# Complex tables of an S5 branch as three wide real products, with roots spread tile by tile and small loads moved to the start

## The chip, the cores and the metric

The kernel runs on one core of one Trainium2 chip, in float32 throughout (matmul operands split into a high and a low part of type float32r, three matmuls for one product). The metric is the device time of one execution in microseconds, the median of several runs. The change is judged by the same time of the changed kernel.

## The reference

One bidirectional encoder layer over two sequences of 512 tokens (the kernel sees them as 1024 rows), D = 1024. The parts that the change touches are the first norm, the u projection and the tables of the state-space branch:

```
h = rms_norm(x, ln1);  q, k, v, u, g_att, g_ssm = split(h @ w_in)
# S5 branch: 2 directions, 64 groups, 64 states, 16 channels a group
dt = exp(log_dt);  A = exp((lam_re + i lam_im) * dt)          # complex, one per (direction, group, state)
B_bar = (A - 1) / lam * (b_re + i b_im)                        # complex, (direction, group, state, 16)
h_t = A * h_(t-1) + B_bar u_t      (forward and backward scan over 512 steps)
y = Re(C h) + d_skip * u
# attention: windowed, with a relative bias by bucket of (key - query): bias = rel_table[bucket]
```

After it come gelu and a gated product, the merge with the attention branch, an output product with residual, a second norm and a squared-ReLU MLP. The change alters none of the results, only how some are reached.

## The kernel before, in words

The scan over 512 steps is cut into 64 chunks of T = 8 steps (`NCHUNK`). For each group the kernel builds, from powers of the complex A, a table `bpre` (B_bar times A^0 to A^7: what a chunk's inputs add to the state) and a table `ctab` (C times A^0 to A^8: what a state adds to the outputs of a chunk, and the lag kernel of a chunk with itself). Real and imaginary part are two planes; the two directions lie in partitions 0 to 63 and 64 to 127.

The stages, in order:

- **Start.** SP loads four rows of x (`x_rows`), two weight columns (`uw_raw`), the transposed x (`x_columns`), then the second sequence. ACT squares each row (`row_root`, L278), POOL takes the power -1/2 of the mean (L280, L281). `spread(s)` (L283 to L289) turns four roots into a 128 x 512 tile of PSUM, where each row holds the root of each token: DVE makes a diagonal of each root, PE multiplies it with ones. `scaled` (L291) multiplies a column of xT by `ln1` and by that tile and splits it in two parts (ACT L296, DVE L297). PE then makes u columns 0 and 1 (L356), with the order of PE, ACT and DVE written by hand (`manual_schedule`). Before that loop DVE computes `dt`, the angle `ang` and its reduction, and the two low parts `uw_lo` of the first weight column, and only then `spread(0)`; `spread(1)` stands at the seam of the two sequences.
- **Powers.** After the loop: sine, exponential, the powers `pr`, `pi` of A by doubling (L379 to L388), the factors `fr`, `fi`, and ten copies on ACT (L402 to L406) into `er`, `ei`, `br_p`, `bi_p`, where each direction has its order of powers.
- **Tables** (`tables(c)`, c = 0 to 7, eight groups each, in two turns q of four groups), with `u_column(2)` and `(3)` ahead and four more u columns between. For each c: SP loads b and c; DVE makes `bb` with negated planes beside it, ACT writes `lbt`. For each turn, six DVE instructions (L474 to L476, twice) make `bpre` and six (L482 to L484, twice) make `ctab`, which goes to `ct_scr` in DRAM. PE multiplies `lbt` with `ctab` (L493, the lag kernel) into a bank of `sps`, ACT copies it to `ks` (L497). SP loads `u_sb`. For each pair of groups PE transposes `bpre` (L506), ACT copies it to `bm` (L508), PE multiplies it with `u_sb` (L513) into another bank of `sps` (two in all), and ACT copies that into the states `h` (L518, L519). At the end of a c DVE adds d_skip on the diagonal (`dg`, L521 to L523) and SP stores `ks` in three transfers to `lag_scr`.
- **Gates and scan.** PE multiplies 13 gate columns (`Gate.whole`, L166, 48 matmuls each); DVE runs the scan over the chunks (L643 to L649, 62 steps of four instructions). After the second gate the bias line is made (one matmul of `rel` with a one-hot, L547) and written to DRAM for all queries (`line_scr`). POOL builds `toep_scr` from `lag_scr` (L554).
- **Read-out** (L741 on): 32 turns, each with loads of `u_sb`, `toep` and `ctab_in` five turns ahead, six matmuls (L686, L688) and a share of three late gates and of the key projection, in an order written by hand.
- Attention, merge and MLP follow, untouched.

Where no order is written, the framework's scheduler orders each engine's queue ahead of the run from its own estimate; at run time each queue (PE, ACT, DVE, POOL, SP) runs in that order, and an instruction that waits holds all behind it. A tile's pool has a number of buffers; the next writer of a buffer waits for the last reader.

Of the kernel before, what the change touches and what calls it, by code (L numbers as in the profile page):

```python
# [63 lines left out]
def hybrid_layer(ctx, tc, x, xT, rel, onehot, ln1, w_qkv, w_ug, q_gain, k_gain, sink, lam_re, lam_im, log_dt,  # L64
# [27 lines left out]
    ct_scr = dram.tile([P, GROUPS, 2, 9 * CH], F32, name="ct_scr")  # L92
# [113 lines left out]
    er = cf.tile([P, 9, GROUPS], F32, name="er")  # L206
    ei = cf.tile([P, 9, GROUPS], F32, name="ei")
    br_p = cf.tile([P, T, GROUPS], F32, name="br_p")
    bi_p = cf.tile([P, T, GROUPS], F32, name="bi_p")
# [3 lines left out]
    lbt = cf.tile([P, 2, SB, 48], F32, name="lbt")  # L213
    with tc.tile_pool(name="xin", bufs=2, reuse_waits="tile") as xin, tc.tile_pool(name="ssmc", bufs=1) as sc:
# [25 lines left out]
        x_rows(0)  # L240
        for c in range(2):
# [6 lines left out]
        SP.dma_start(dd[32:48, :], d_skip)  # L248
        SP.dma_start(bglu_sb, b_glu)
# [33 lines left out]
        def spread(s):  # L283

            ps = spread_ps[s] = sps()
            for i in range(4):
                dg = xin.tile([P, P], F32, tag="rs_diag", name="rs_diag", bufs=4)
                V.tensor_scalar_mul(dg, ident, root[s * 4 + i])
                PE.matmul(ps[:, i * P:(i + 1) * P], ones, dg, start=True, stop=True)  # L289
# [25 lines left out]
        with tc.manual_schedule(engines={mybir.EngineType.PE, mybir.EngineType.Activation, mybir.EngineType.DVE}):  # L315
            exp_exact(dt, ldt)
            den, nr, tn = c64("den"), c64("nr"), c64("tn")
            V.tensor_mul(den, lr, lr)
            V.tensor_mul(tn, li, li)
            V.tensor_add(den, den, tn)  # L320
            V.reciprocal(den, den)
            V.tensor_mul(ang, li, dt)
            V.tensor_scalar(kk, ang, 1.0 / (2.0 * math.pi), ROUND_MAGIC, op0=ALU.mult, op1=ALU.add)
            V.tensor_scalar_add(kk, kk, -ROUND_MAGIC)
            for part in (TWO_PI_1, TWO_PI_2, TWO_PI_3):
                V.scalar_tensor_tensor(ang, kk, -part, ang, op0=ALU.mult, op1=ALU.add)
            V.tensor_scalar(ang, ang, -3.1415925, 3.1415925, op0=ALU.max, op1=ALU.min)
            for t in range(4):
                row_root(t)
            w_los = [weight_half(raw[:, i * KT // 2:(i + 1) * KT // 2, :], w, i) for raw, w in first_w for i in range(2)]  # L330
            w_los.pop(0)()
            w_los.pop(0)()
            spread(0)
            owed = [scaled(0, 0)]
            out_ps = {}
            for s in range(NSEQ):
                for c in range(2):
                    out_ps[c, s] = acc()
                for k in range(KT):
                    if k + 1 < KT:  # L340
                        owed.append(scaled(s, k + 1))
                    elif s == 0:
                        spread(1)
# [14 lines left out]
            for fn in w_los:  # L358
                fn()
            sn, sh = c64("sn"), c64("sh")  # L360
# [40 lines left out]
            for src, e_t, b_t in ((pr, er, br_p), (pi, ei, bi_p)):  # L401
                S.copy(e_t[0:64, 0:8, :], src[0:64, 1:9, :])  # L402
                S.copy(e_t[64:128, 0:8, :], src[64:128, 8:0:-1, :])
                S.copy(e_t[:, 8, :], src[:, 0, :])
                S.copy(b_t[0:64, :, :], src[0:64, 7::-1, :])
                S.copy(b_t[64:128, :, :], src[64:128, 0:8, :])  # L406
        for c in range(2):
            u_store(c, ups[c])
        V.tensor_scalar_mul(gain_q, gain_q, HD ** -0.5)
        V.tensor_scalar_mul(nsink, nsink, -1.0)  # L410
# [4 lines left out]
    if True:  # L415
# [4 lines left out]
        for ri in range(2):  # L420
            for s in range(NSEQ):
                for half, n in ((slice(0, 64), 7), (slice(64, 128), 0)):
                    S.copy(a8r[half, ri, :, s], er[half, n, :])
                    S.activation(a8i[half, ri, :, s], ei[half, n, :], AF.Copy, scale=-1.0 if ri == 0 else 1.0)
# [10 lines left out]
        with tc.tile_pool(name="ssmt", bufs=2) as sp:  # L435
            def tables(c):
# [3 lines left out]
                bx = sp.tile([P, 3, SB, CH], F32, tag="bx", name="bx")  # L440
                cx = sp.tile([P, 3, SB, CH], F32, tag="cx", name="cx")
                SP.dma_start(bx[:, 1], b_re[:, gs, :])
                SP.dma_start(bx[:, 2], b_im[:, gs, :])
                SP.dma_start(cx[:, 0], c_re[:, gs, :])
                SP.dma_start(cx[:, 1], c_im[:, gs, :])
                bb = sp.tile([P, 3, SB, CH], F32, tag="bb", name="bb", bufs=1)
                tw = sp.tile([P, 2, SB, CH], F32, tag="tb", name="tw", bufs=1)
                V.tensor_scalar_mul(bx[:, 0], bx[:, 2], -1.0)
                V.tensor_mul(tw, bx[:, 0:2], fi[:, None, gs, None].to_broadcast([P, 2, SB, CH]))
                V.tensor_mul(bb[:, 1:3], bx[:, 1:3], fr[:, None, gs, None].to_broadcast([P, 2, SB, CH]))  # L450
                V.tensor_add(bb[:, 1:3], bb[:, 1:3], tw)
                V.tensor_scalar_mul(bb[:, 0], bb[:, 2], -1.0)
                V.tensor_scalar_mul(cx[:, 1], cx[:, 1], -1.0)
# [1253 lines left out]
```

## Time and profile before

| | |
|---|---|
| median of 3 runs | 1565.12 us (1564.83 to 1565.55) |
| profiled execution, device time | 1567.3 us |
| its span, first to last instruction | 1565.5 us |
| mean granted TensorE clock | 0.988 |
| busy PE / PEld / DVE / ACT / POOL | 1489.8 / 1270.1 / 1125.5 / 769.1 / 125.4 us |

PE is TensorE's matmuls, PEld its weight loads, DVE VectorE, ACT ScalarE, POOL GpSimd, SP the queue that issues most transfers. A row of the groups reads: line, engine, operation, output and inputs, shapes, number of instructions, busy us, mean ns of one, then the engine's idle time just before them and what ended it. A float32 matmul appears as two passes.

### The profile page before, as it was taken

The numbers are of one execution on the slowest core, as the hardware profiler recorded it, in microseconds if no ns is written. First come the engines' busy times: TensorE is split into PE (matmuls) and PEld (weight loads), VectorE is DVE, ScalarE is ACT, GpSimd is POOL, SyncE is SP. The second block draws the span as 40 slices with busy tenths as digits, with TensorE's granted clock in tenths as the row PEclk, the third lists the DMA queues.
The fourth block names the chain that finished last, engine by engine and source line by source line (L and its number), as shares of the span: only waits on it lengthen the run. The fifth ranks groups of instructions, "written<-read, shape, count | busy, mean of one in ns | idle before, by whom it ended". The sixth has DMA issues, their size and how long they took to land.

```text
span 1565.5 us, 22224 instructions
## 1 busy us (share of the span) xinstructions
PE 1489.8 (95%) x8058; PEld 1270.1 (81%) x8058; DVE 1125.5 (72%) x2015; ACT 769.1 (49%) x1379; POOL 125.4 (8%) x222
## 2 busy tenths in 40 slices
PE   5999999999999999999899998999999999999998
PEld 3777778888999888897689986888888788888787
DVE  6898987995454888888784577777777578566553
ACT  5577763214334877777443344555455434433332
POOL 1000002000022233331100100000000000000000
PEclk9999999999999999999899998999999999999999
DMA  7443549427852332224954232444444694455332
GB/s 258 127 146 124 156 138 298 145 94 254 259 191 60 89 95 62 83 84 151 304 203 176 81 115 101 155 149 148 151 158 155 233 346 143 152 159 163 121 121 67
DMA packets 122713, 243.38 MB, mean 155 GB/s; under 512 B 16315, under 2 KB 47163, under 8 KB 122604
## 3 DMA queue, kind: packets, MB, share of 16 engines
q1 hardware_dynamic: 97564, 186.24, 37.5%
q10 hardware_dynamic: 22480, 46.25, 7.9%
q0 software_dynamic: 2560, 9.48, 1.9%
q8 instruction: 63, 1.03, 0.3%
q14 instruction: 46, 0.38, 0.1%
HBM read 172.68 MB, written 81.82 MB: 163 GB/s over the span
## 4 chain that ended last, share of the span: by engine, by line
PE 71%; DVE 15%; ACT 5%; DMA 4%; issue 3%; SPq 0%; POOL 0%; ACTq 0%; DVEq 0%
PE bank L128 13%; PE bank L129 13%; PE bank L127 13%; PE acc L593 5%; PE acc L622 5%; PE acc L166 4%; PE acc L128 2%; PE acc L127 2%; PE acc L129 2%; PE sps L688 2%; DMA c_raw<-in_w_ug_dram 2%; PE sps L493 2%; PE acc L356 2%; PE sps L513 1%; DVE h L649 1%
## 5 line engine op out<-in xcount | busy, mean ns | idle before, releaser
L127 PE MATMUL bank<-b_hi,a_hi 128*128 128x512 f32 x448 | 174.4, 392 | 3.9 <-ACT b_hi L1581 3.9
L128 PE MATMUL bank<-b_lo,a_hi 128*128 128x512 f32 x448 | 175.7, 392 | 2.1 <-DVE b_lo L1582 2.0
L129 PE MATMUL bank<-b_hi,a_lo 128*128 128x512 f32 x448 | 175.3, 391 | 0.0
L593 PE MATMUL acc<-w_hi,hT 128*128 128x256 f32 x768 | 165.0, 292 | 0.0
L166 PE MATMUL acc<-hT,c_hi 128*128 128x512 f32 x512 | 164.0, 397 | 0.0
L1581 ACT CAST a_hi<-d_a 128x1024 fp32r<-128x1024 f32 x56 | 58.9, 1052 | 182.0 <-PE bank L128 178.0
L1582 DVE TENSOR_TENSOR a_lo<-d_a,a_hi 128x1024 fp32r<-128x1024 f32 x56 | 68.5, 1224 | 107.3 <-ACT a_hi L1581 107.3
L593 PEld LDWEIGHTS acc<-w_hi,hT 128*128 128x128 f32 x768 | 128.0, 190 | 3.5
L166 PEld LDWEIGHTS acc<-hT,c_hi 128*128 128x128 f32 x512 | 96.2, 189 | 20.4 <-issue 1.5
L593 PE MATMUL acc<-w_lo,hT 128*128 128x256 f32 x384 | 108.6, 283 | 0.2 <-DVE w_lo L588 0.2
L127 PE MATMUL bank<-act,u_hi 128*128 128x512 f32 x256 | 101.1, 395 | 7.1 <-DVE a L1422 7.1
L127 PEld LDWEIGHTS bank<-b_hi,a_hi 128*128 128x128 f32 x448 | 84.5, 189 | 21.8 <-ACT b_hi L1581 4.3
L128 PEld LDWEIGHTS bank<-b_lo,a_hi 128*128 128x128 f32 x448 | 84.6, 189 | 21.1 <-DVE b_lo L1582 3.6
L166 PE MATMUL acc<-hT,c_lo 128*128 128x512 f32 x256 | 101.2, 395 | 0.0
L128 PE MATMUL bank<-act,u_hi 128*128 128x512 f32 x256 | 100.8, 394 | 0.0
L129 PE MATMUL bank<-act,u_lo 128*128 128x512 f32 x256 | 100.7, 393 | 0.0
L129 PEld LDWEIGHTS bank<-b_hi,a_lo 128*128 128x128 f32 x448 | 84.6, 189 | 17.5
L882 ACT ACTIVATE p<-p,nmx 128x257 f32<-128x257 f32 (+1 forms) x128 | 72.2, 564 | 35.8 <-DVE nmx L876 35.7
L1434 ACT CAST u_hi<-s 128x512 fp32r<-128x512 f32 x64 | 39.8, 623 | 74.4 <-PE bank L128 53.3
L593 PEld LDWEIGHTS acc<-w_lo,hT 128*128 128x128 f32 x384 | 73.4, 191 | 1.0 <-DVE w_lo L588 0.4
L876 DVE CUSTOM_DVE_ANT_0 p<-sps,bias,nsink 128x256 f32<-128x256 f32 (+1 forms) x128 | 69.1, 541 | 2.1 <-PE sps L872 0.3
L1582 DVE TENSOR_TENSOR b_lo<-k,b_hi 128x1024 fp32r<-128x1024 f32 x56 | 68.2, 1218 | 1.1 <-ACT b_hi L1581 1.1
(333 smaller groups left out, 3763.4 us busy)
## 6 DMA issues: line engine op xcount, KB each, us to landing
d_a<-a_scr SPq DMA_DIRECT2D x56, 512.0 KB
u_raw<-in_w_up_dram SPq DMA_DIRECT2D x32, 512.0 KB
a_scr<-t ACTq DMA_DIRECT2D x64, 256.0 KB
k<-in_w_down_dram SPq DMA_DIRECT2D x32, 512.0 KB
a_scr<-a ACTq DMA_DIRECT2D x48, 256.0 KB
c_raw<-in_w_ug_dram SPq DMA_DIRECT2D x44, 256.0 KB
ct_scr<-ctab SPq DMA_DIRECT2D x16, 576.0 KB
ctab_in<-ct_scr SPq DMA_DIRECT2D x32, 288.0 KB
```

The lines of the kernel that those rows point to most:

```text
L127: PE.matmul(ps, a[0], b[0], start=first, stop=False)
L128: PE.matmul(ps, a[0], b[1], start=False, stop=False)
L129: PE.matmul(ps, a[1], b[0], start=False, stop=last)
L166: PE.matmul(self.ps[s], self.w[p == 2][:, k, :], hT[s][p == 1][:, k, :], start=i % (3 * KT) == 0, stop=i % (3 * KT) == 3 * KT - 1)
L356: PE.matmul(out_ps[c, s], first_w[c][1][p == 2][:, k, :], hT[s][p == 1][:, k, :], start=k + p == 0, stop=k == KT - 1 and p == 2)
L593: PE.matmul(ps, act[p == 2][:, k, col:col + P], self.w[k // 4][p == 1][:, k % 4, :], start=i == 0, stop=i == 3 * KT - 1)
L622: PE.matmul(self.ps[s], w_g[self.m][p == 2][:, k, :], y_part(s, int(p == 1), k), start=k + p == 0, stop=k == KT - 1 and p == 2)
L876: V.tensor_tensor_reduce(self.p[:, h, 1:1 + self.nk], self.s[h][:, 0:self.nk], biases[self.j][h][:, b0:b0 + self.nk], -1.0, nsink[:, hh:hh ...
L882: S.activation(p, p, AF.Exp, bias=self.nmx[:, h:h + 1], scale=-1.0, accum_out=self.sums[:, h, self.qb:self.qb + 1])
L1434: S.copy(hi, src)
L1581: S.copy(hi, src)
L1582: V.tensor_sub(lo, src, hi.bitcast(F32))
```

## The change

- **Tables.** The powers are kept as planes beside each other: `e2` and `b2` hold imaginary and real power for each turn of four groups, `e_s` their difference, `b_s` their sum. `complex_table` then makes both planes of a table by three instructions: one product over both planes (1024 or 1152 wide), one product of one plane's width (512 or 576), and one addition over both planes. For that DVE prepares `bk` and `ck` (differences of real and imaginary parts) for each c, instead of negated planes. `ctab` and `ct_scr` hold the plane outside the group; the read-out loads two groups from there as two runs.
- **Lag kernel.** It has a PSUM bank of its own (`ps_o`). `ks` holds four groups and is stored after each turn; `dg` and its addition run on POOL. `u_sb` is loaded by two groups.
- **Start.** `spread` takes one tile; three spreads stand right behind their roots, the fourth after four small instructions on `den`; the second sequence's four stand at k = 5 of the first. The reduction of the angle follows the loop. The casts of the two first weight columns alternate. The bias line's loads, matmul and copy stand in the start. b and c of the first two c are loaded behind x, the later ones two c ahead.
- The scaling of `gain_q` and `nsink` moves into the read-out.

```
+    e2 = cf.tile([P, 9, GROUPS // SG, 2, SG], F32, name="e2")
+    b2 = cf.tile([P, T, GROUPS // SG, 2, SG], F32, name="b2")
+    e_s = cf.tile([P, 9, GROUPS], F32, name="e_s")
+    b_s = cf.tile([P, T, GROUPS], F32, name="b_s")
...
+    def b_and_c(c):
+        bx = ssmb.tile([P, 2, SB, CH], F32, tag="bx", name="bx")
+        cx = ssmb.tile([P, 2, SB, CH], F32, tag="cx", name="cx")
+        for i, (b_, c_) in enumerate(((b_re, c_re), (b_im, c_im))):
+            SP.dma_start(bx[:, i], b_[:, gs, :])
+            SP.dma_start(cx[:, i], c_[:, gs, :])
...
         x_rows(0)
+        SP.dma_start(rel_sb[0:N_BUCKETS, :], rel)
+        SP.dma_start(oh_sb, onehot)
...
         SP.dma_start(dd[32:48, :], d_skip)
+        bc_tiles = {c: b_and_c(c) for c in range(2)}
...
-        def spread(s):
-            ps = spread_ps[s] = sps()
-            for i in range(4):
-                V.tensor_scalar_mul(dg, ident, root[s * 4 + i])
-                PE.matmul(ps[:, i * P:(i + 1) * P], ones, dg, start=True, stop=True)
+        def spread(t):
+            if t % 4 == 0:
+                spread_ps[t // 4] = sps()
+            V.tensor_scalar_mul(dg, ident, root[t])
+            PE.matmul(spread_ps[t // 4][:, t % 4 * P:(t % 4 + 1) * P], ones, dg, start=True, stop=True)
...
+            ps = tps()
+            PE.matmul(ps[0:N_HEADS, :], rel_sb, oh_sb, start=True, stop=True)
             exp_exact(dt, ldt)
+            for t in range(4):
+                row_root(t)
+                if t < 3:
+                    spread(t)
             V.tensor_mul(den, lr, lr)
...
+            spread(3)
+            w_los = [weight_half(...) for i in range(2) for raw, w in first_w]
+            S.copy(ln_sb, ps[0:N_HEADS, :])
+            GP.dma_start(line_one, ln_sb)
-            w_los.pop(0)()
-            w_los.pop(0)()
-            spread(0)
...
+                    if w_los and k == 0:
+                        w_los.pop(0)()
+                    if s == 0 and k == 5:
+                        for t in range(4, 8):
+                            spread(t)
...
+            for pl, src in ((1, pr), (0, pi)):
+                sv = src.rearrange("p n (q g) -> p n q g", g=SG)
+                S.copy(e2[0:64, 0:8, :, pl], sv[0:64, 1:9])
...
+            V.tensor_sub(e_s..., ev[:, :, 1], ev[:, :, 0])
+            V.tensor_add(b_s..., bv[:, :, 1], bv[:, :, 0])
...
+                bx, cx = bc_tiles.pop(c)
+                if c + 2 < KT:
+                    bc_tiles[c + 2] = b_and_c(c + 2)
...
-                    for ri in range(2):
-                        V.tensor_mul(bpre[:, ri], bc_pow(br_p, T), bc_ch(bb[:, 1 + ri], T))
-                        V.tensor_mul(tb[:, :, 0:T, :], bc_pow(bi_p, T), bc_ch(bb[:, ri], T))
-                        V.tensor_add(bpre[:, ri], bpre[:, ri], tb[:, :, 0:T, :])
...
+                    def complex_table(out, powers, total, planes, first, n):
+                        V.tensor_mul(out..., powers (both planes, over the channels), planes (both, over n))
+                        V.tensor_mul(tb[:, :, 0:n, :], total (over the channels), first[:, ql] (over n))
+                        V.tensor_add(ov, ov, tv[:, None].to_broadcast([P, 2, SG, n * CH]))
+                    complex_table(bpre, b2, b_s, bk, bb[:, 0], T)
+                    complex_table(ctab, e2, e_s, ck, cx[:, 0], 9)
+                    ks = sp.tile([48, SG, 9, CH], F32, tag="ks", name="ks", bufs=1)
-                        ps = sps()
+                        ps = ps_o.tile([P, 512], F32, tag="po", name="lag")
...
+                    GP.tensor_tensor(dg[32:48], ..., op=ALU.mult)
+                    GP.tensor_tensor(ks[32:48, :, 8, :], ks[32:48, :, 8, :], dg[32:48], op=ALU.add)
+                    SP.dma_start(lag_scr[:, gl, 8:15, :], ks[0:16, :, 0:7, :])
+                    SP.dma_start(lag_scr[:, gl, 0:7, :], ks[16:32, :, 1:8, :])
+                    SP.dma_start(lag_scr[:, gl, 7, :], ks[32:48, :, 8, :])
                     for gp in range(SG // SH):
+                        u_sb = sp.tile([P, SH, NSEQ * NCHUNK], F32, tag="u_sb", name="u_sb")
+                        SP.dma_start(u_sb, u_scr[:, :, gu:gu + SH].rearrange("t c g k -> (t c) g k"))
...
-            SP.dma_start(ctab.rearrange("p g r n -> p (g r n)"), ct_scr[:, g0:g0 + SH]...)
+            SP.dma_start(ctab, ct_scr[:, q // 2, :, q % 2 * SH:(q % 2 + 1) * SH, :])
```

More of the change, by code (lines that the diff above doesn't have):

```diff
@@ L459, in tables @@
+                S.copy(lbt[0:64, :, :, 0:16], bb[0:64])
+                S.copy(lbt[64:128, :, :, 16:32], bb[64:128])
+                S.copy(lbt[:, :, :, 32:48], bb)
                 for q in range(SB // SG):
@@ L539, in hybrid_layer @@
             if i == 1:
-                rel_sb = evp.tile([N_BUCKETS + 1, N_HEADS], F32, tag="ev", name="rel_sb")
-                GP.memset(rel_sb, NEG_INF)
-                SP.dma_start(rel_sb[0:N_BUCKETS, :], rel)
-                oh_sb = evp.tile([N_BUCKETS + 1, LINE], F32, tag="ev", name="oh_sb")
-                SP.dma_start(oh_sb, onehot)
-                ps = tps()
-                PE.matmul(ps[0:N_HEADS, :], rel_sb, oh_sb, start=True, stop=True)
-                ln_sb = evp.tile([N_HEADS, LINE], F32, tag="ev", name="ln_sb")
-                S.copy(ln_sb, ps[0:N_HEADS, :])
-                GP.dma_start(line_one, ln_sb)
                 GP.dma_start(line_scr, line_one[:, None, :].to_broadcast([N_HEADS, P, LINE]))
@@ L687, in read_out @@
                 for ri in range(2):
-                    PE.matmul(o, ctab[:, gi, ri, 0:T * CH], st[:, ri, g].rearrange("p s k -> p (s k)"),
+                    PE.matmul(o, ctab[:, ri, gi, 0:T * CH], st[:, ri, g].rearrange("p s k -> p (s k)"),
                               start=False, stop=ri == 1)
```

140 lines of the change are left out of this document (68 added, 72 removed).

## The prediction

> **What bounds the kernel now.** I read four views in this order: the page's first part (which engine is full), the table of stretches (where TensorE is not full), the groups of instructions inside the stretch that the change rewrites, and the chain and timeline at the stretch's two ends.
>
> ```profile
> span 1565.5 us, 22224 instructions
> PE 1489.8 (95%) x8058; PEld 1270.1 (81%) x8058; DVE 1125.5 (72%) x2015; ACT 769.1 (49%) x1379; POOL 125.4 (8%) x222
> ```
>
> TensorE is busy for 95% of the span, so work taken from VectorE only counts where TensorE waits for it. The stretches (columns: from:to, length, busy time of PE, PEld, DVE, ACT, POOL with instructions, granted clock, DMA share, GB/s):
>
> ```profile
> 0.00:18.30 18.30, 2.07 (x8) 1.78 (x8) 9.84 (x38) 8.78 (x15) 3.83 (x14) 1.00 0.88 314
> ...
> 47.70:235.80 188.10, 177.31 (x1034) 141.52 (x1033) 163.17 (x322) 131.01 (x210) 0.42 (x2) 1.00 0.46 142
> 235.80:355.00 119.20, 119.20 (x524) 97.54 (x522) 106.53 (x269) 27.97 (x47) 7.83 (x10) 1.00 0.51 174
> 355.00:360.20 5.20, 1.94 (x14) 1.82 (x13) 2.30 (x4) 1.87 (x2) 0.00 (x0) 0.91 0.92 316
> 360.20:415.00 54.80, 54.80 (x335) 48.88 (x335) 24.07 (x34) 20.71 (x37) 0.00 (x0) 0.98 0.82 261
> ```
>
> The five rows are: the start before the first projection matmul; the tables of the S5 branch with u columns 2 to 7; the scan on DVE beside the gate matmuls on PE; the step to the read-out; the read-out. After 360.2 PE is full, and the change alters no matmul there. So all it can win lies before 360.2.
>
> How much does PE lose in the tables stretch? Its busy time overlaps and includes the drain of each matmul, so I count by pitch, from runs in the chain that nothing interrupts (start, length, what, how many passes):
>
> ```profile
> 77.79 0.89 PE tps L506 x8
> ...
> 83.99 1.60 PE sps L493 x12
> 85.59 1.98 PE sps L513 x16
> ...
> 235.81 7.75 PE acc L166 x34
> ```
>
> That is 0.111, 0.133, 0.124 and 0.228 us a pass. The counts between 47.7 and 354.9:
>
> ```profile
> L166 PE MATMUL acc<-hT,c_hi 128*128 128x512 f32 x416 | 131.3, 393 | 0.0
> ...
> L493 PE MATMUL sps<-ctab,lbt 128*48 128x144 f32 x256 | 38.9, 291 | 9.6 <-ACT h L519 7.2 <-DVE ctab L484 1.7 <-ACT up L432 0.6
> ...
> L127 PE MATMUL acc<-hT,c_hi 128*128 128x512 f32 x96 | 38.4, 400 | 0.0
> ...
> L513 PE MATMUL sps<-u_sb,bm 128*128 128x128 f32 x256 | 32.4, 280 | 1.1 <-ACT ks L497 1.1
> L506 PE MATMUL tps<-ident,bpre 128*128 128x128 f32 x128 | 18.4, 276 | 0.2
> ```
>
> Gates: 416 passes on c_hi are two thirds of 624, times 0.228 is 142.3. Six u columns: three lines of 96, 288 x 0.228 = 65.7. Tables: 256 x 0.133 + 256 x 0.124 + 128 x 0.111 = 80.0. Together 288 us of pitch in the 307.3 us from 47.7 to 355.0: **19 us of PE idle**, all before 235.8, since the second stretch is full (524 x 0.228 = 119.5 in 119.2). These 19 us are the ceiling for the tables part. DVE is busy 163 of 188 us there, the nearest to full after PE, and paces the tables.
>
> **The change part by part.** (1) The tables on DVE. One row of each kind, and a 1024-wide row for the new width (mean ns after the busy time):
>
> ```profile
> L1582 DVE TENSOR_TENSOR a_lo<-d_a,a_hi 128x1024 fp32r<-128x1024 f32 x56 | 68.5, 1224 | 107.3 <-ACT a_hi L1581 107.3
> ```
> ```profile
> L484 DVE TENSOR_TENSOR ctab<-ctab,tb 128x576 f32<-128x576 f32 x32 | 24.1, 754 | 0.4
> ...
> L476 DVE TENSOR_TENSOR bpre<-bpre,tb 128x512 f32<-128x512 f32 x32 | 22.0, 687 | 0.4
> ...
> L451 DVE TENSOR_TENSOR bb<-bb,tw 128x256 f32<-128x256 f32 x8 | 3.4, 422 | 0.1
> ```
>
> Before, a turn q makes six products of 512 and six of 576: 6 x 0.687 + 6 x 0.754 = 8.65 us. After, `bpre` takes 1024 + 512 + 1024 and `ctab` 1152 + 576 + 1152. From 512 to 1024 costs 0.537 us, so 1152 is 1.224 + 128 x 0.00105 = 1.36: 2 x 1.22 + 0.69 + 2 x 1.36 + 0.75 = 6.60. Saved 2.05 a turn, 33 us over 16 turns. The preparation per c keeps three 256-wide products' worth (one of them in two halves), trades four small negations for four small differences, and sends the `dg` product and the addition into `ks` to POOL: about level, +1 to -2 us in all; I take 0. Once, two additions `e_s` and `b_s` of 576 and 512 wide (1.4 us) and the moved angle reduction (seven 64-wide instructions) stand before the first table. They cost nothing while PE works on u columns 2 and 3, 96 passes of 0.228 = 21.9 us from 47.7 on; bare they would cost under 3 us. b and c come with x, so the first table no longer waits for them behind the u stores.
>
> What do 33 us of DVE buy? At least nothing (PE's order may stall elsewhere), at most the 19 us. The waits of PE's weight loads say where half of the idle is:
>
> ```profile
> PEld sps L493 <- ACT h L519: 9.7, 9, 1.9
> ```
>
> The lag matmul L493 takes the bank `sps` and waits until ACT has emptied it of the state products. The change gives it a bank of its own (`ps_o`). The other half is turnaround between DVE, PE and ACT, whose instructions on ACT are unchanged (131 us busy before; with the stage near 150 us ACT is near 85%). I take the row's size, **-9.5**, ends 0 and -19.
>
> (2) Longer queues. `ks` is now one buffer per turn instead of one per c, so its three stores, the POOL addition and the lag bank go round every turn; SP gets five more issues per c (three stores, two `u_sb`), 40 in all, and `u_sb` is half as deep. On SP these lie beside PE's 150 us; cost 0 while they come in time, priced as rivals B and C if not.
>
> (3) The start (timeline: start, us, engine, what, and the idle before it):
>
> ```profile
> 11.54 0.57 POOL L281 TENSOR_TENSOR rs<-ss,neg_half 128x1 f32<-128x1 f32 x1
> ...
> 11.68 2.38 ACT L301 CAST uw_hi<-uw_raw 128x512 fp32r<-128x512 f32 x4 [0.53 <-DMA uw_raw<-in_w_ug_dram]
> ...
> 13.20 1.28 DVE L302 TENSOR_TENSOR uw_lo<-uw_raw,uw_hi 128x512 fp32r<-128x512 f32 x2
> ...
> 14.40 0.87 DVE L288 TENSOR_SCALAR rs_diag<-ident,rs 128x128 f32<-128x128 f32 x4
> ...
> 16.85 1.41 DVE L294 SCALAR_TENSOR_TENSOR rn_xn<-xc,ln_sb,sps 128x512 f32<-128x512 f32 x2 [1.58 <-PE sps L289]
> ...
> 18.30 2.43 PE L356 MATMUL acc<-hT,uw_hi 128*128 128x512 f32 x4 [1.49 <-ACT hT L296]
> ...
> 32.13 0.71 PE L356 MATMUL acc<-hT,uw_hi 128*128 128x512 f32 x2
> ...
> 36.87 0.96 PE L356 MATMUL acc<-hT,uw_hi 128*128 128x512 f32 x3 [1.63 <-ACT up L313]
> ```
>
> The last root is there at 12.1, its spread waits until 14.40 behind the two `uw_lo`. Now three spreads go ahead of it and one remains: xn at 13.4 instead of 16.85. But ACT ends the four casts at 14.1 (0.6 each) and then copies `ln_sb`, taken at a cast's 0.6 too, before the cast of xn; so the first matmul moves from 18.3 to about 15.5, and two `uw_lo` (2 x 0.64) now stand behind it on DVE: -2.0 remains. The second spread moves from the seam of the sequences (PE stands for most of 32.8 to 36.9) into k = 5; the wait for the bank that ACT copies at L313 stays: -1.5 of those 4.0. Together **-3.5**, ends 0 (the DMA share is 0.88 up to 18.3: columns of x landing late) and -6. The bias line's matmul lies in PE's empty start, two more loads stand ahead of `uw_raw` on SP and eight ahead of the gains and of column 2, which has slack until k = 3 of the second sequence.
>
> (4) The step to the read-out:
>
> ```profile
> 353.12 1.28 DVE L159 TENSOR_TENSOR c_lo<-c_raw,c_hi 128x512 fp32r<-128x512 f32 x2
> ...
> 353.83 0.93 SPq L157 DMA_DIRECT2D c_raw<-in_w_ug_dram  x2
> ...
> 354.99 2.89 SPq L660 DMA_DIRECT2D toep<-toep_scr  x5
> ...
> 358.41 0.46 PE L686 MATMUL sps<-u_sb,toep 128*128 128x128 f32 x2 [3.26 <-DMA toep<-toep_scr]
> ```
>
> DVE finishes the scan at 353.1 and only then makes `c_lo`; SP's weight load waits for that, and the five `toep` loads behind it on SP's queue come late. PE stands 3.3 us and runs at 0.91 clock through the stretch 355 to 360.2. With the tables over near 205, a scan of the same 107 us ends near 313, while PE has gates until about 342: `c_lo` and `toep` are early. **-4.5** (ends 0 and -5.2).
>
> (5) The read-out's `ctab_in` now gathers two runs of 1152 B a partition instead of one of 2304. Prices from the DMA totals of 340 to 460 and of 0 to 45 (packets, MB, share of 16 engines):
>
> ```profile
> q1 hardware_dynamic: 15264, 20.68, 54.8%
> ```
> ```profile
> q1 hardware_dynamic: 4864, 10.40, 63.2%
> ```
>
> 68.9 ns at 1355 B and 93.6 ns at 2138 B: 26 ns a packet plus 0.0315 a byte. 128 more packets are 0.21 us of sixteen engines a turn, 6.7 over 32 turns; the share of 0.82 becomes about 0.89, still hidden. **+1**, ends 0 and +6.7. DMA: Bandwidth & Descriptors in the Trainium skill (section Why small descriptors are slow) gives about 3 cycles a packet beside one per 32 bytes; by that the split adds 4% to these loads, an estimate near 0, and the sum would be 1 us lower.
>
> Sum: -3.5 - 9.5 - 4.5 + 1 = -16.5. The profiled execution took 1567.3 us (span 1565.5 and 1.8 around it) and becomes 1550.8; the runs' median, 1565.12, lies 2.2 lower: 1548.6, said as **1549**.
>
> **The rivals.** B: the ring of `ks` holds the tables at their old pace. POOL's addition must run between DVE's long products, and a POOL instruction beside such a one is stretched:
>
> ```profile
> 21.90 0.69 DVE L297 TENSOR_TENSOR hT<-rn_xn,hT 128x512 fp32r<-128x512 f32 x1
> 21.91 0.76 POOL L280 TENSOR_SCALAR ss<-ss 128x1 f32<-128x1 f32 x1 [9.80 <-ACT rn_junk L278]
> ...
> 23.77 0.22 POOL L280 TENSOR_SCALAR ss<-ss 128x1 f32<-128x1 f32 x1 [0.46 <-ACT rn_junk L278]
> ```
>
> 0.76 instead of 0.22 when it starts with the two-input subtraction; behind a 1.36 us product it may take 1.4, and three stores with their landing follow before ACT may write `ks` again. SBUF — State Buffer in the Trainium skill (section Who interferes with whom) says the same of two-input VectorE instructions and GpSimd reads: one waits for the whole of the other. The row agrees. If the ring takes the old turn (the stretch less u columns 2 and 3, 188.1 - 21.9 = 166 us over 16, 10.4 us), the stage keeps its length, the scan its end, the step its stall: -3.5 + 1, 1562.6. Against it: with four groups a turn the ring has three such waits in 10.4 us.
>
> C, the other side: one lag bank and one `ks` make PE wait in its own order for ACT's copy, twice a turn. The stage idles 1.2 us a turn now; if the round by ACT behind its state copies leaves 2.2, that is 35 instead of 19, +16, the step's gain is lost, the head's -3.5 and +1 stay: +13, about 1578; it turns slower above 1.3 us a turn. Against it: the scheduler can put u columns, gates and transposes between.
>
> D: the whole 19 us go, with -5.2 and -3.5: 1565 - 27.7 = 1537. E: the read-out turns DMA bound: 1549 + 5.7 = 1555.
>
> **How the numbers follow.** Forecast 0.60 (its own range 1543 to 1555), B 0.12, C 0.11, D 0.09, E 0.08. The range 1537 to 1563 takes in all but C: 0.89, and less for the tails. 0.2% is 3.1 us, about what a measurement here tells from no change: faster 0.77 (forecast, D, E), same 0.12 (B), slower 0.11 (C).
>
> **What the profile after would show.** Six groups of 512 and 576 become wide ones of about 1.22 and 1.36 us, and DVE's tables end near 205. L493's wait for `h` is gone; a wait of it for `ks`, or of ACT's `ks` copy for a store, would be C or B. The first projection matmul near 15.5, no stop of 3.3 us before L686, gates on PE until about 342. The prediction is wrong if the scheduler's new order of PE leaves as much idle as now, or if the read-out turns take more than the present pace.

## The result and the profile after

The changed kernel took 1588.34 us (median of 4 runs, 1586.39 to 1591.56) where the kernel before took 1565.34 beside it: a ratio of 1.014 with an interval of 1.011 to 1.017. It was forecast at 1549 and faster. Spans below are 1588.3 us after and 1565.5 before, 22.8 apart. The kernels of the experiments ran in several sessions, so they are compared by their ratio to the kernel before, run beside each of them.

The page's first part of the changed kernel:

```profile
span 1588.3 us, 22242 instructions
PE 1501.1 (95%) x8058; PEld 1279.7 (81%) x8058; DVE 1104.3 (70%) x1913; ACT 767.5 (48%) x1379; POOL 148.0 (9%) x254
```

VectorE does 21 us less in 102 fewer instructions. The time rose nevertheless. The stretches of the same run (start, tables, scan and gates, read-out; columns as before):

```profile
0.00:17.80 17.80, 3.91 (x11) 1.95 (x11) 7.48 (x30) 9.29 (x16) 5.05 (x16) 1.00 0.80 274
17.80:58.10 40.30, 30.62 (x105) 23.06 (x106) 26.42 (x50) 16.80 (x30) 4.04 (x9) 0.87 0.74 267
58.10:246.50 188.40, 168.38 (x954) 135.84 (x953) 139.61 (x222) 126.63 (x206) 23.20 (x33) 0.94 0.42 128
246.50:382.30 135.80, 135.80 (x600) 112.44 (x599) 111.36 (x278) 31.11 (x53) 6.11 (x8) 1.00 0.43 145
382.30:437.00 54.70, 54.70 (x345) 49.04 (x344) 23.82 (x33) 22.51 (x39) 0.00 (x0) 1.00 0.88 270
```

Read it against the five rows of before. The projection of the head ends at 57.8 instead of 47.7 (the first weight load of column 2): 10.1 us. From the first matmul of column 2 to the last state product the tables take 188.4 us, as long as before (187.8 from that matmul at 48.0 on; the row of before starts at 47.7), although VectorE is busy 139.6 us in them instead of 163.2. TensorE too does less there: 954 instructions for 1034. The 80 that are missing are gate matmuls, and they come back in the next row: 600 for 524 passes, 135.8 us for 119.2. The stop before the read-out is gone, as forecast. The read-out begins at 382.3 for 358.4, 23.9 us later, which is the whole loss: 10.1 at the head, 0.6 in the tables' length and 13.2 in the stretch behind them (135.8 for 122.6 up to the first matmul of the read-out). The groups in the tables' stretch:

```profile
L524 PE MATMUL lag<-ctab,lbt 128*48 128x144 f32 x256 | 41.6, 309 | 9.8 <-ACT lbt L491 4.4 <-ACT ks L528 3.0 <-issue 2.1
L554 PE MATMUL sps<-u_sb,bm 128*128 128x128 f32 x256 | 38.2, 301 | 5.0 <-ACT bm L549 4.8
...
L498 DVE TENSOR_TENSOR ctab<-e,ck 128x1152 f32<-128x1152 f32 x16 | 21.8, 1361 | 15.7 <-PE lag L524 12.7 <-DMA ct_scr<-ctab 3.0
L510 DVE TENSOR_TENSOR ctab<-ctab,tb 128x1152 f32<-128x1152 f32 x16 | 21.7, 1356 | 0.4
L547 PE MATMUL tps<-ident,bpre 128*128 128x128 f32 x128 | 21.1, 303 | 5.3 <-ACT bm L549 5.3
L510 DVE TENSOR_TENSOR bpre<-bpre,tb 128x1024 f32<-128x1024 f32 x16 | 19.8, 1236 | 0.2
L498 DVE TENSOR_TENSOR bpre<-b,bk 128x1024 f32<-128x1024 f32 x16 | 19.8, 1236 | 7.0 <-PE tps L547 7.0
```

The wide products cost what was worked out for them (1.24 and 1.36 us). But the waits have turned round. Before, TensorE's lag set waited for ACT's `h`; now TensorE waits for ACT at each of its three steps (`lbt`, `ks`, `bm`), and VectorE, no longer the pace, waits 19.7 us for TensorE to free `ctab` and `bpre`. One such place on ACT, and then on TensorE (timeline of after):

```profile
204.65 1.02 ACT L559 COPY h<-sps 64x504 f32<-64x504 f32 x1
205.68 1.02 ACT L560 COPY h<-sps 64x504 f32<-64x504 f32 x1
206.71 0.40 ACT L491 COPY lbt<-bb 128x256 f32<-128x256 f32 x1
207.14 1.04 ACT L559 COPY h<-sps 64x504 f32<-64x504 f32 x1
208.19 1.02 ACT L560 COPY h<-sps 64x504 f32<-64x504 f32 x1
209.24 1.07 ACT L549 COPY bm<-tps 128x512 f32<-128x512 f32 x2
```
```profile
207.17 1.40 PE L524 MATMUL lag<-ctab,lbt 128*48 128x144 f32 x8 [1.92 <-ACT lbt L491]
209.88 1.97 PE L547 MATMUL tps<-ident,bpre 128*128 128x128 f32 x8 [1.31 <-ACT bm L549]
```

Four copies of the states, 1 us each, which nobody waits for yet, stand in ACT's queue ahead of the `bm` copies that TensorE waits for.

To compare runs I use one figure, TensorE's idle time in the tables by pitch, as in the prediction: the stretch less 145.7 us (six u columns 65.7, tables 80.0) less 0.228 us for each gate pass that lies in it. Before, that is 187.8 - 145.7 - 104 x 0.228 = 18.4 us; after, 188.4 - 145.7 - 25 x 0.228 = 37.0. The forecast had it fall by 9.5.

Not all of the 37.0 us is standing still, since the figure counts every pass at the pitch of the full clock. Eight passes of the lag kernel's matmul took 1.18 us and, eleven microseconds later, eight others took 2.15, where the granted clock was 0.50 (timeline of after, then a stretch of it):

```profile
200.86 1.18 PE L524 MATMUL lag<-ctab,lbt 128*48 128x144 f32 x8
...
211.77 2.15 PE L524 MATMUL lag<-ctab,lbt 128*48 128x144 f32 x8
```
```profile
208.00:220.00 12.00, 9.29 (x37) 6.66 (x36) 11.31 (x15) 3.34 (x7) 2.25 (x2) 0.50 0.44 137
```

TensorE's busy time times the missing share of the granted clock, summed over stretches of 2 us, gives an estimate of what slower passes add in the tables: 10.0 us in after and 0 before (and 6.1 in `e3`, 10.9 in `e5`, 1.7 in `e9`, 0 in `e10`, the runs below). So of the 18.6 us that came on top, about 8.6 are more waiting and 10 are slower passes.

### The profile page after: what moved, and what is told of

The parts are those of the page before. It is cut to its first block, busy times and chain, and to the rows that moved or that the text cites. A ratio compares the mean times of both kernels' runs of the same rounds, so it can differ in the third digit from the quotient of the medians.

```text
span 1588.3 us, 22242 instructions
## 1 busy us (share of the span) xinstructions
PE 1501.1 (95%) x8058; PEld 1279.7 (81%) x8058; DVE 1104.3 (70%) x1913; ACT 767.5 (48%) x1379; POOL 148.0 (9%) x254
## 3 DMA queue, kind: packets, MB, share of 16 engines
q8 instruction: 63, 1.03, 0.3%
## 4 chain that ended last, share of the span: by engine, by line
PE 67%; DVE 10%; ACT 5%; issue 3%; DMA 3%; POOL 0%; SPq 0%; DVEq 0%; ACTq 0%; POOLq 0%
PE bank L128 13%; PE bank L129 12%; PE bank L127 12%; PE acc L166 11%; PE acc L616 5%; PE sps L710 2%; PE acc L129 2%; PE acc L127 2%; PE acc L128 2%; DVE pl L921 1%; DVE p L900 1%; ACT p L906 1%; PE sps L708 1%; PE lag L524 1%; DVE qa L875 1%
## 5 line engine op out<-in xcount | busy, mean ns | idle before, releaser
L166 PE MATMUL acc<-hT,c_hi 128*128 128x512 f32 x512 | 160.0, 392 | 0.0
L127 PE MATMUL acc<-w,act 128*128 128x256 f32 (+1 forms) x224 | 68.2, 304 | 1.2 <-ACT w L1208 1.2
```

What stands on the lines that cost most here:

```text
L127: PE.matmul(ps, a[0], b[0], start=first, stop=False)
L166: PE.matmul(self.ps[s], self.w[p == 2][:, k, :], hT[s][p == 1][:, k, :], start=i % (3 * KT) == 0, stop=i % (3 * KT) == 3 * KT - 1)
```

## The experiments

**First set: head alone, ring alone, both loads mended, products narrow again.** `e1_head_only` is the kernel before with the whole start of the change. `e2_ring_only` has only the lag bank, `ks`, `dg` and `u_sb` of the change:

```
+                    ks = sp.tile([48, SG, 9, CH], ..., bufs=1)      # inside the turn
-                        ps = sps()
+                        ps = ps_o.tile([P, 512], F32, tag="po", name="lag")
+                    GP.tensor_tensor(dg..., op=ALU.mult); GP.tensor_tensor(ks..., dg..., op=ALU.add)
+                    SP.dma_start(lag_scr...)  x3, each turn;  u_sb by pairs of groups
```

> The kernel before with the start of the changed one alone (spread by tile, bias line in the start, b and c of two c's loaded behind x), tables and lag kernel as before. Theory H (the bias line's 4 MB copy and the eight small loads delay column 2's weights and stop PE for about 8 us): 1570 us, some 5 above before, and the stop shows before the last low part of column 2. Rival (the start is an advantage as forecast, all the loss is in the tables): 1561.5 us.

> The kernel before with the lag kernel's part of the change alone: bank of its own, ks by turn with three stores, dg and its addition on POOL, u_sb by two groups; tables by twelve instructions and the start as before. Theory R (the ring of ks, POOL, SP and stores, and the lag bank, hold the tables stage): 10 to 20 us slower than before, 1575 to 1585. Rival (the ring is hidden; the loss comes from the wide products and what their order does): within 3 us of before.

`e1` gave 1.0049 (1.0031 to 1.0066): its head ends at 65.3, 17.6 us late, and a part of that is won back since the stop before the read-out is gone. So the start loses by itself, some 8 us where theory H had 5. `e2` gave 0.9994 (0.9983 to 1.0006), with the idle at about 21 us (fourteen lag passes run behind the end of its stretch): the smaller ring, the GpSimd addition and the extra stores cost nothing. TensorE's lag set, matmuls and weight loads together, waits 16.7 us for `ks` there, where it waited 16.9 us for `h` before. The prediction's rivals B and C were the ring's, and in that form they fall.

`e3_head_fix` is the changed kernel with bias line and b and c loads back where they were; `e4_narrow` is the changed kernel with six narrow products for each table in place of three wide ones:

```
-            ln_sb, line_one in the start;  bc_tiles ahead of the gains          (e3)
+            the same behind the second gate;  bc_tiles behind column 2's weights
-                    V.tensor_mul(both planes) ; tb ; V.tensor_add(both planes)   (e4)
+                    for r in range(2): V.tensor_mul(plane r) ; tb ; V.tensor_add(plane r)
```

> The changed kernel with the bias line back behind the second gate and the first b and c loaded behind column 2's weights. Theory H: no stop of PE near 43 to 50 us, 7 to 9 us less than the changed kernel, about 1580. Rival (the start's stop has another cause): 1588.

> The changed kernel with each table again by six instructions of one plane's width (512 or 576), so that DVE works 33 us more in the tables; all else as changed. Theory R (DVE no longer paces the tables): within 4 us of the changed kernel, 1588. Rival (DVE still paces the tables): 15 us or more above it, 1603 or more.

`e3` gave 1.0026 (1.0012 to 1.0041): its head ends at 44.5, earlier than before, yet it is no faster than before. Both of its cases were missed: it is some 18 us faster than after, where 7 to 9 or nothing were expected. `e4` gave 1.0075 (1.006 to 1.009): with 27 us more of VectorE's work in the tables than after it is faster than after, by some 10 us, which neither of its cases had. Its idle is about 30 us (fourteen lag passes lie behind the stretch), with 77 gate passes in the stretch. So there are two losses, one at the head and one in the tables, and the second is smaller without the very products that were to win there. The narrow products alone do not bring it back to before, though: `e1`, with narrow products and the whole new start, has 17.2 us of idle and `e2` 21. What else in the change costs the other 9 us (by the same estimate 4.2 of `e4`'s idle are slower passes) is not isolated.

**Which load stops the head?** In the changed kernel POOL sends the bias line for all queries at 22.87; before, it did so at 247.70, under the gates:

```profile
247.70 1.02 POOL L551 DMA_DIRECT2D line_scr<-line_one  x1 [0.97 <-DMA line_one<-ln_sb]
```
```profile
22.87 1.06 POOL L574 DMA_DIRECT2D line_scr<-line_one  x1 [5.12 <-DMA line_one<-ln_sb]
...
27.31 0.33 SPq L222 DMA_DIRECT2D bx<-in_b_re_dram  x1
28.26 0.33 SPq L223 DMA_DIRECT2D cx<-in_c_re_dram  x1
30.58 0.33 SPq L222 DMA_DIRECT2D bx<-in_b_im_dram  x1
32.40 0.33 SPq L223 DMA_DIRECT2D cx<-in_c_im_dram  x1
...
46.13 0.90 SPq L327 DMA_DIRECT2D c_raw<-in_w_ug_dram  x2
49.45 0.62 ACT L320 CAST c_hi<-c_raw 128x512 fp32r<-128x512 f32 x1 [10.50 <-DMA c_raw<-in_w_ug_dram]
50.10 0.69 DVE L321 TENSOR_TENSOR c_lo<-c_raw,c_hi 128x512 fp32r<-128x512 f32 x1 [10.77 <-ACT c_hi L320]
...
51.45 1.22 PE L378 MATMUL acc<-hT,uw_hi 128*128 128x512 f32 x2 [7.85 <-DVE hT L316]
```

The copy writes 16 x 128 x 512 values of 4 bytes, 4.2 MB. Behind it SP's small loads leave at 2 us each, and column 2's weights (`c_raw`), the last in SP's queue, leave at 46.1. ACT stands 10.5 us for them, VectorE, whose order has their split ahead of the next `hT`, 10.8, and TensorE 7.9. Two kernels take back one cause each:

```
-            GP.dma_start(line_one, ln_sb) ...  in the start            (e5: line back behind the gates)
-        bc_tiles = {c: b_and_c(c) for c in range(2)}                   (e6: b and c behind column 2's weights)
```

> The changed kernel with the bias line alone back behind the second gate; b and c still come with x. The changed kernel stands at 1.014 of before, the one with both moved at 1.0026. Theory L (the copy of the line to 4 MB, which the POOL queue starts at 23 us, is what delays x and column 2's weights): 1.003 to 1.006 of before. Rival S (the eight small loads ahead of column 2's weights on SP's queue do it): 1.010 to 1.014.

> The changed kernel with the first b and c loaded behind column 2's weights; the bias line stays in the start. Theory L: 1.010 to 1.014 of before, PE's stop stays. Rival S: 1.003 to 1.006, PE's stop is gone.

`e5` gave 1.0081 (1.0057 to 1.0104), `e6` 1.0107 (1.0092 to 1.0122); the head ends at 46.1 and 54.7. `e6` is theory L's case. `e5` lies between the two cases: its head comes back, but its time is above theory L's 1.003 to 1.006, since its tables took 198.6 us (see under "Open" below). In `e5` the same small loads leave at 0.6 us each, and the weights at 32.4 (timeline, then its second ten microseconds of the head: TensorE 8.53 busy, DMA share 0.58; in after, two stretches between 30 and 50):

```profile
25.78 0.34 SPq L222 DMA_DIRECT2D bx<-in_b_re_dram  x1
26.40 0.33 SPq L223 DMA_DIRECT2D cx<-in_c_re_dram  x1
...
32.41 0.91 SPq L321 DMA_DIRECT2D c_raw<-in_w_ug_dram  x2
```
```profile
26.30:36.30 10.00, 8.53 (x40) 6.64 (x40) 9.15 (x18) 6.18 (x13) 0.82 (x2) 1.00 0.58 187
```
```profile
30.00:40.00 10.00, 9.77 (x36) 7.65 (x37) 8.88 (x15) 4.60 (x8) 0.66 (x2) 0.83 1.00 369
40.00:50.00 10.00, 3.59 (x16) 2.56 (x14) 0.00 (x0) 0.55 (x2) 0.00 (x0) 0.88 0.50 146
```

So the 4.2 MB copy is the head's cause. Without it `e5`'s head ends 11.7 us earlier than in after and already holds seven passes of column 2 (the first at 39.55), 1.6 us by pitch, so it is as good as `e3`'s, 13.3 us earlier. The early b and c cost nothing there; on top of the copy they add 3.1 us (57.8 for 54.7). The rest of the change at the start is worth having. `e7_good_head` is the kernel before with only the spread tile by tile, the order of the casts and the late angle:

> The kernel before with only the roots spread tile by tile, the casts of the two columns alternating and the angle's reduction behind the loop; bias line, b, c and tables as before. Theory H (without the two transfers the start gives the forecast 3.5 us): 0.9975 of before (3 to 5 us less). Rival (the seam and the start are paced by x's landing): 1.000.

It gave 1563.22 us, 0.9971 (0.9958 to 0.9983), with the first projection matmul at 15.2 and the head's end at 43.3. `e8_gates_56` asked whether the tables only lack fill: it is `e3` with two gates written between tables 4 and 5 and between 6 and 7.

```
+                for i in early.get(c, ()):        # early = {4: (0,), 6: (1,)}
+                    gates[i].whole()
```

> The changed kernel with bias line and b, c loads moved as before, and two gate columns written into the program between tables(4) and (5) and between (6) and (7), so that PE's queue holds 115 gate matmuls before the last table matmul instead of 22. Theory O (the tables lose because the scheduler, with shorter products, leaves PE's queue without gates to fill the waits for ACT): 10 to 15 us less than without, 0.993 to 0.997 of before. Rival (the gates only push the tables back and the scan ends later): 1.002 to 1.005.

It missed both cases: 1.0067 (1.0048 to 1.0086). The idle fell to 22.4 us, but the stretch grew to 194.5; the scan on VectorE ended later by that, and TensorE stood before the read-out again (117.9 us busy of 132.6). More fill is not enough; the tables themselves must end sooner.

**Order or work?** `e9_by_hand` keeps `e3`'s instructions on their engines and writes the order of TensorE, ACT and VectorE in this stage by hand; `e10_bm_dve` leaves the order to the scheduler and moves one copy:

```
+            with tc.manual_schedule(engines={PE, Activation, DVE}):            (e9)
+                for i in range(turns):
+                    lag(i, 0); turn_b(i, 0); fill(4); lag(i, 1); turn_b(i, 1)
+                    products(i + 1); fill(5)
+                    state(i, 0); fill(4); state(i, 1); fill(5)
-                        S.copy(bm.rearrange("p r g n -> p (r g n)"), ps)         (e10)
+                        V.tensor_copy(bm.rearrange("p r g n -> p (r g n)"), ps)
```

> e3_head_fix (wide products, bias line and b and c loaded where they were before) with the stage of the tables in an order written by hand for TensorE, ScalarE and VectorE: in each of the 16 turns two lag sets, two transposes and two state sets with 4, 5, 4 and 5 matmuls of u columns 4 to 7 and of the first two gates between them, VectorE one turn ahead, ScalarE taking ks and bm of a half before h. The instructions are the same. Theory O (the length of the stage is a matter of the queues' order, in which TensorE, ScalarE and VectorE wait for each other in a ring): TensorE's work in the stage is 163.7 us in e3 and its waits 22; with fill at every wait the stage should fall to about 170 us with the same 24 to 30 gate passes in it, and the kernel to 0.985 to 0.992 of before. Rival S (a single buffer or ScalarE's own work sets a turn, whatever the order: 123.5 us busy in 186, and lag, ks and bm in line): the stage stays at 183 us or more, and the kernel at 0.999 or above.

> e3_head_fix with one line changed: the 32 copies of the transposed b table (bm, 0.587 us each on ScalarE, 17.3 us in e3) are made by VectorE; the planner orders the rest as it will. ScalarE falls from 123.5 to about 106 us in the stage, VectorE rises from 139 to about 158. If ScalarE's queue is what TensorE's transposes and state matmuls wait for (8.3 us for state matmuls and 3.2 for transposes behind bm in e3), those 11 us go and the stage falls from 186 to about 176: 0.996 of before or less. If the order on TensorE sets it, as theory O says, the waits only move (bm now stands behind the wide products on VectorE, 1.2 to 1.4 us each, where it stood behind h): 1.000 to 1.006.

Both gained: `e9` 1553.77 us, 0.9895 (0.9871 to 0.9918), `e10` 1555.15 us, 0.9900 (0.9872 to 0.9928). The tables' stretch of `e3`, of `e9` and of `e10`:

```profile
44.80:230.90 186.10, 163.71 (x952) 133.54 (x951) 138.81 (x220) 123.53 (x204) 26.82 (x33) 0.96 0.42 129
```
```profile
44.20:222.30 178.10, 172.50 (x1021) 139.79 (x1020) 141.27 (x221) 130.43 (x211) 23.82 (x35) 0.99 0.45 141
```
```profile
44.40:221.10 176.70, 168.96 (x1001) 136.31 (x1000) 155.49 (x254) 114.20 (x179) 34.32 (x34) 1.00 0.46 141
```

In `e9` ACT does more than in `e3` (130.4 us) in 8 us less. So neither ACT's load nor a single buffer held `e3`: the order of the queues did. Its idle falls from 35.2 to 11.4 us (slower passes are 6.1 of the one and 1.7 of the other), its stage by 8 us and not by the 16 expected, but 69 more gate passes lie in it; VectorE still waits ten times, 19.6 us in all, for TensorE's transposes. `e10` comes close to it (14.6 us) by taking `bm` out of ACT's queue, where it stood behind `h`. The groups of `e10`, where TensorE's waits for `bm` are gone:

```profile
L544 PE MATMUL sps<-u_sb,bm 128*128 128x128 f32 x249 | 33.4, 280 | 0.6 <-ACT h L550 0.4 <-DMA u_sb<-u_scr 0.3
...
L539 DVE COPY bm<-tps 128x512 f32<-128x512 f32 x32 | 21.5, 685 | 6.6 <-PE tps L537 4.8 <-PE sps L544 1.7
L537 PE MATMUL tps<-ident,bpre 128*128 128x128 f32 x128 | 17.4, 274 | 0.2
```

VectorE is busy 155.5 us in it, nearly as much as before: the freed time is what pays for `bm`.

**Do the wide products play a part at all, do the two losses add, and are the two mendings one?** `e11_narrow_bm` is `e7` with that one line of `e10`, `e12_after_bm` the changed kernel with it, `e13_by_hand_bm` is `e9` with it.

> The twelve narrow products of the kernel before, with the good head (e7_good_head), and the bm copies on VectorE as in e10. If the wide products are what lets e10 gain, this must not gain: VectorE's work in the stage of the tables would be 164.4 + 32 x 0.685 = 186 us, more than the 177 to 190 that the stage takes, so VectorE sets it, the stage stays at 188 to 195 us, and the time is 0.997 to 1.003 of before. Rival: the bm copies behind h were all that held e3, and the width of the products plays no part: 0.990 to 0.993, as e10.

> The changed kernel itself, bias line and loads at the head left in, with the bm copies on VectorE and nothing else. Loss at the head and loss in the tables are two things: after to e3 by mending the head was 1.014 to 1.0026, and e3 to e10 by the bm copies 1.0026 to 0.990. If they add, this is 0.999 to 1.004 of before, with PE standing 8 to 10 us before 58 us as in after and a stage of tables of about 177. If the two share a cause (VectorE late after the head), it is above 1.006 or below 0.996.

> e9_by_hand with the bm copies on VectorE. In e9 PE stands 5.6 us in 178.1 and VectorE waits 19.6 us for transposes, behind bm on ScalarE. If the two mendings are the same one (bm soon after its transposes), nothing is left to gain: 0.987 to 0.991. If ScalarE's h copies still hold lag sets in e9, a few us more: 0.984 to 0.987.

`e11` gave 1.0098 (1.0076 to 1.0119): no gain, and a larger loss than the 1.003 expected at most. TensorE's idle in the tables is small (15.0 us), but VectorE is busy 181 of 199.5 us, its scan ends late, and TensorE stands 25 us before the read-out:

```profile
44.10:243.60 199.50, 193.28 (x1101) 154.58 (x1100) 181.22 (x360) 119.50 (x187) 2.22 (x4) 0.99 0.45 139
243.60:373.20 129.60, 104.55 (x455) 84.62 (x455) 107.67 (x270) 26.88 (x43) 6.01 (x8) 0.93 0.47 162
```

With `e7`, `e3` and `e10` this makes a square (ratios to before). `e3` and `e10` also have the change's ring and lag bank, which were worth nothing in `e2`, and load b and c two c ahead, as `e1` does with 17.2 us of idle.

| | `bm` copied by ACT | `bm` copied by VectorE |
|---|---|---|
| narrow products | 0.9971 (`e7`) | 1.0098 (`e11`) |
| wide products | 1.0026 (`e3`) | 0.9900 (`e10`) |

Each half of the pair loses alone, and together they gain: the wide products 2.0% where VectorE has `bm` as well, and minus 0.55% where it has not. Against `e7` the pair is worth 0.7%.

`e12` gave 0.9999 (0.9990 to 1.0009), as expected of two losses that add: its head has the same hole, its tables are `e10`'s.

```profile
40.00:50.00 10.00, 3.50 (x14) 2.56 (x13) 2.13 (x4) 1.28 (x3) 0.00 (x0) 0.83 0.45 126
```
```profile
56.40:235.30 178.90, 170.38 (x1001) 137.26 (x1000) 155.59 (x254) 113.87 (x179) 34.33 (x33) 0.99 0.45 140
```

`e13` missed both of its cases: 1.0120 (1.0103 to 1.0137), the stage 211.6 us. Its longest waits of VectorE and TensorE:

```profile
DVE bm L550 <- PE tps L548: 35.7, 19, 4.2
...
PE tps L548 <- DVE bpre L506: 17.8, 14, 1.8
```

The order of `e9` lets VectorE work a turn ahead. With `bm` written into VectorE's queue ahead of the next turn's products, VectorE must wait for TensorE's transposes first, and TensorE then for VectorE. An order fits one assignment of work; the same line that is worth 1.3% in the scheduler's order costs 2.2% in this one.

## Why the prediction was wrong

By its own steps, in us of the profiled executions:

| step | forecast | after | with its fault mended |
|---|---|---|---|
| tables: idle of TensorE | -9.5 | +18.6, of it about 10 slower passes | -3.8 in `e10`, -7.0 in `e9` |
| ring, queues | 0 | 0 (`e2`) | |
| start: end of the head | -3.5 | +10.1 | -4.4 in `e7`, -3.2 in `e3` |
| stop before the read-out | -4.5 | gone, -3.3 | gone in `e10` |
| read-out | +1 | -1.6 | |

The column of after sums to +23.8, where the spans differ by 22.8.

**Step (1), "what do 33 us of DVE buy", failed.** Its two ends, 0 and -19, left out a loss. It named as reason for the lower end that TensorE's order may stall elsewhere, and then took the waiting row's own size. Two things were missed. VectorE at 163 of 188 us was the nearest to full, but the 33 us could be used only if the chain behind it, TensorE's transposes, ACT's `bm`, TensorE's states, ran a turn faster, and ACT's queue was not looked at in order, only by its busy time (131 us, "near 85%"). And the scheduler places gates into this stage by what its own estimate leaves free; 76 to 80 passes went out of it, some 17 us, when the estimate saw shorter tables. That "the scheduler can put u columns, gates and transposes between" was used as an argument against rival C; that it can as well take them out was not priced. The closing sentence, "if the scheduler's new order of PE leaves as much idle as now", named the right danger, with no chance and no price given to it; it left twice as much. What the scheduler's estimate holds was not seen; only its orders were. Nor had any term the granted clock, which is by the estimate above about half of the +18.6. The 33 us themselves were mis-sized too: VectorE's busy time in the stretch fell by 23.6, and its tables ended at 232.6 (230.2 before) where 205 was forecast. The sum went by the rows' means, and these overlap: in the timeline of before a `bpre` product at 218.97 lasts 0.68 us and the next instruction starts 0.61 later, so fewer instructions save less than their means; how much of the gap that is was not worked out.

**Step (3) failed by one transfer.** The prediction counted the bias line's matmul, its copy on ACT and two loads on SP. It did not count what `line_scr` sends: the move took 4.2 MB from under the gates to the one stretch where the DMA share was 0.88 to 0.94 and the next weights were due. It also gave column 2 "slack until k = 3" behind eight loads; with the engines full each of them took 2 us on SP, and the slack was gone. The rest of the step held: with the line away `e7` begins at 15.2 where 15.5 was forecast.

**Step (4) came out, but not by its road.** The stop is gone: VectorE's `c_lo` begins at 342.8, and SP's `toep` leaves at 356.5, 26 us ahead of the read-out. But the step counted on a scan that ends near 313, and the scan ended at 360.1, later than before (353.2):

```profile
342.78 0.68 DVE L159 TENSOR_TENSOR c_lo<-c_raw,c_hi 128x512 fp32r<-128x512 f32 x1
...
356.47 2.22 SPq L683 DMA_DIRECT2D toep<-toep_scr  x5
...
359.69 0.42 DVE L672 TENSOR_TENSOR h<-tt 128x256 f32<-128x256 f32 x1
```

The scheduler had put `c_lo` between two steps of the scan, and TensorE had gates until 382.3, among them the passes that had left the tables. That the stop is gone is luck for this step: it goes in `e1` too, whose tables are as before. In `e10` the scan does end sooner, at 338.7.

**Step (5) held** in its mechanism: the DMA share of the read-out is 0.88 (0.89 was worked out, 0.82 before), still hidden; TensorE is busy through the whole of it. The 32 turns took 95.3 us for 96.9, at a granted clock of 1.00 for 0.98, which is the whole difference; so the +1 was nothing and rival E falls.

**Rival B's stretched GpSimd instruction is there and costs nothing.** The addition into `ks`, 16 x 64 elements, takes 0.753 us in the mean, and `dg` of the same size 0.678, where one `dg` at 58.33 took 0.34. The Trainium skill (SBUF — State Buffer, section Who interferes with whom) has a GpSimd instruction that reads SBUF and a VectorE instruction with two SBUF inputs exclude each other; the rows agree with that, but GpSimd waits for ACT for 123 us of the stage, so it had the time.

**Rival C's picture, TensorE waiting in its own order for ACT, is nearest to what happened**, but mainly through `bm` behind `h` (10.1 us of TensorE's waits in the groups of after, for 4.4 of `lbt` and 3.0 of `ks`) and less through the lag bank and `ks`, as `e2` and `e10` show. That its 16 us are near the 18.6 measured is luck, since about 10 of these are the clock, which it did not have. With both faults mended and VectorE's time put to use, `e10` and `e9` reach 0.990 and 0.9895, which by its size is the forecast's -16.5 us (0.9895 of 1567); 10.4 us of `e10`'s are there when its read-out starts (348.0 for 358.4). This is an agreement of size alone: it takes an edit that the forecast did not have, and the tables give 3.8 and 7.0 us of the 9.5.

Open: about 11 to 15 us of idle stay in the tables in the best kernels; and `e5` and `e3`, whose tables hold the same instructions, took 198.6 and 186.1 us for them. Of the 12.5 us, 27 more gate passes are 6.2 and slower passes 4.8 (10.9 for 6.1), and `e5`'s profiled run took 5.7 us more than its median; why the scheduler orders the two so differently no run explains.

## What to carry to other kernels

Time taken from the busiest engine of a stage is worth something only if the queue behind it can deliver sooner: read the next engine's queue in order (what stands ahead of the copy that TensorE waits for), not its busy share alone, and ask where the freed time will be used; here moving one copy onto the engine that had been relieved turned a loss into a gain. When filler work is placed by a scheduler, price the case that a shorter stage keeps its length and pushes its filler out. Read the granted clock beside idle time that is counted by pitch, because slow passes look like waits in it. When a block of code is moved, follow it to its last transfer and count the bytes against the DMA share of the place that it moves to.

## What the runs showed of the hardware

- Small loads on SP's queue leave at 0.6 us each in `e5` and at about 2 us each in after, where the 16 DMA engines are at a share of 1.00 to 1.03.
- The granted clock of TensorE falls around its stops: 0.83 and 0.88 in the two stretches of after shown above, 0.83 in `e12`, and 0.94 over the whole of after's tables, where `e10` has 1.00. Behind the stop of 7.9 us it was 0.56 from 50 to 55 us, so the stop cost more than itself. The Trainium skill (TensorE: Matmul & The Clock Gate, section HAM oscillation — how this bites in real kernels) warns of idle gaps above about 3.4 us; the 7.9 us stop agrees. In after's tables the clock was 0.50 from 208 to 220 us, around waits of only 1.92 and 1.31 us (before 207.17 and 209.88), so there the measurement goes beyond the page. No run here fixes the length of a wait at which the clock falls.
- One 128 x 512 copy out of PSUM takes 0.587 us on ACT and 0.685 us on VectorE.
